# Gate and up of an inner tile as seven block products, and four rounds of inner tiles, in three feed-forward stages

## The chip, the cores and the metric

The kernel runs on one core of a Trainium2 chip. The metric is the device time of one execution in microseconds; three runs of the kernel before gave a median of 2734.63 us (2733.28 to 2737.92). The profile and the trace below come from one further execution with the profiler on.

## What is computed

Two transformer blocks on 512 tokens of width 1024, in float32. The first has two layers, and each layer has two feed-forward stages, one ahead of and one behind its mixing (a recurrent one in layer 0, windowed attention in layer 1). That makes four feed-forward stages, numbered 0 to 3. The second block follows stage 3. What matters here, cut from the reference:

```python
D_MODEL, SEQ, D_FF = 1024, 512, 2816

def swiglu(x, w_in, w_out):
    gate, up = jnp.split(x @ w_in, 2, axis=-1)
    return (jax.nn.silu(gate) * up) @ w_out

h = h + 0.5 * rms_norm(swiglu(rms_norm(h, g[0]), ffn_w_in[layer, 0], ffn_w_out[layer, 0]), g[1])
...
h = h + 0.5 * rms_norm(swiglu(rms_norm(h, g[4]), ffn_w_in[layer, 1], ffn_w_out[layer, 1]), g[5])
```

## The kernel before

Every large product keeps float32 accuracy by splitting both factors into a high part in the reduced format fp32r and a low rest. `weights` loads 128x1024 numbers of weights (512 KB, by a DMA issued on SyncE, into one of three raw buffers `wr`); ScalarE copies them to the high part (L153) and VectorE subtracts to get the low part (L154), both into one of five buffers `whl`. `mm3` then makes three matmuls for each block of weights: high by high, high by low, low by high (L164 to L166). Tokens lie along the free axis (512 columns, or two halves of 256), features along the partitions, in `KT` = 8 blocks of 128. The normalised tokens are held as `xn[k]`, scaled by the norm's gain and split; the norm's own factor per token, `rx`, is multiplied in behind the product.

`ffn` is one feed-forward stage; stages 0, 2 and 3 run through it (stage 1 is woven into the recurrent mixing by the class `Halves`, which stays). The 2816 inner features are 22 inner tiles of 128, worked in two rounds (`fh`) of `FH` = 11. An inner tile is gate and up: 2 x 8 blocks x 3 matmuls of 512 columns into two PSUM banks `gu`. `act` turns them into the inner activation: gate and up by `rx` on VectorE (L328, L329), Silu on ScalarE (L330), their product on VectorE (L331), and the split into `a` (L267 on ScalarE, L268 on VectorE). The first three tiles of a stage (`nsp`) run on the two token halves one after the other, since the second half of the tokens is still being normalised by the tail of the step before (`self.tail`).

After the eleven tiles of a round come the output products (`dtile`): 8 output tiles of 128 features, each 11 blocks x 3 matmuls into a PSUM bank `o`. Round 0 is copied by ScalarE into the buffers `m` (L393), round 1 is added to them by VectorE (L395), and the squares for the norm behind are summed. In round 1 the last five output tiles (four in stages 1 and 2) run on the two token halves apart, so that half 0 can be normed (`postnorm`, and then `after_half`: the next norm and the first work of the next stage) while TensorE makes half 1. The norm takes two small matmuls on TensorE: a sum over the partitions (`st<-ones,acc`, L175) and a spread of the factor (`st<-dg,ones`, L186).

Work of other stages that waits for nothing is fed in step by step as side generators (`ada` in stage 0; `kv_gain` and `angles` in stage 2). Each engine runs its instructions in order; the order is made by the scheduler of the Tile framework, which places the instructions that the code issues by a timeline of its own.

## Time and profile before

| | |
|---|---|
| median of 3 runs | 2734.63 us |
| profiled execution | 2736.7 us, of which the span is 2735.0 us |
| instructions | 43654 |
| TensorE busy | 2638.4 us, 96% |
| VectorE busy | 1472.2 us, 54% |
| ScalarE busy | 1154.1 us, 42% |
| GpSimd busy | 118.6 us, 4% |
| DMA | 344.2 MB, 126 GB/s over the span |

PE is TensorE, DVE is VectorE, ACT is ScalarE, POOL is GpSimd, SP is SyncE. Busy time is summed over the span. Matmuls are pipelined, so the durations that are listed for them overlap, and the distance of two starts says what one costs. A row of a stretch ends with the granted clock (1.00 is full), the DMAs' busy share and GB/s. In other rows, `out<-in` names the tiles, and L154 is line 154.

### The profile page before, as it was taken

To read this page: it belongs to the slowest core of one execution; us is meant where nothing else is said; L and a number is where in the kernel's file an instruction comes from. 1 tells how busy PE (TensorE), PEld (TensorE's weight loads), DVE (VectorE), ACT (ScalarE), POOL (GpSimd) and SP (SyncE) were. 2 spreads that over 40 slices of the span, in tenths; PEclk is the share of its full clock that TensorE was granted. 3 is DMA by queue.
4 is the path that set the end of the run, shared out by engine and by line. 5 is a ranking of instruction groups with operands and counts; after the bars stand their busy time and mean duration, and the time that the engine had idled before them with its cause. 6 is when DMAs were issued, how large, how long until landed. Compare 5 with 4: busy or idle time off the path is not lost.

```text
span 2735.0 us, 43654 instructions
## 1 busy us (share of the span) xinstructions
PE 2638.4 (96%) x17326; PEld 2288.5 (84%) x17326; DVE 1472.2 (54%) x2992; ACT 1154.1 (42%) x2061; POOL 118.6 (4%) x148
## 2 busy tenths in 40 slices
PE   8999988899999999999999999899999999999998
PEld 7888887778788999999988889679888898767777
DVE  7724456565548556448652446547524456235655
ACT  5223315345355554345532234446322334345542
POOL 0000000000000000000000000340000000001300
PEclk9999999999999999999999999999999999999999
DMA  6632316864666463235442333102323233113352
GB/s 206 213 109 93 108 49 217 239 186 136 184 196 169 131 205 127 93 109 179 131 149 94 99 109 128 47 24 87 114 93 97 96 103 122 54 52 100 116 184 82
DMA packets 207556, 344.20 MB, mean 126 GB/s; under 512 B 66164, under 2 KB 136180, under 8 KB 207352
## 3 DMA queue, kind: packets, MB, share of 16 engines
q1 hardware_dynamic: 206920, 341.13, 39.9%
q8 instruction: 136, 2.23, 0.4%
q14 instruction: 68, 0.56, 0.1%
q10 hardware_dynamic: 432, 0.28, 0.0%
HBM read 298.51 MB, written 41.26 MB: 124 GB/s over the span
## 4 chain that ended last, share of the span: by engine, by line
PE 85%; DVE 5%; DMA 4%; issue 3%; ACT 3%; SPq 0%; POOL 0%; DVEq 0%; ACTq 0%; POOLq 0%
PE gu L164 12%; PE gu L165 12%; PE gu L166 12%; PE o L164 8%; PE o L166 8%; PE o L165 8%; PE ps L594 4%; PE ps L164 2%; PE ps L166 2%; PE ps L165 2%; PE psg L164 1%; PE psg L166 1%; PE psg L165 1%; PE z L1783 1%; DMA kk<-kk 1%
## 5 line engine op out<-in xcount | busy, mean ns | idle before, releaser
L153 ACT ACTIVATE whl<-wr 128x1024 fp32r<-128x1024 f32 x417 | 439.7, 1059 | 727.9 <-PE gu L166 400.6
L154 DVE TENSOR_TENSOR whl<-wr,whl 128x1024 fp32r<-128x1024 f32 x417 | 508.2, 1222 | 368.3 <-ACT whl L153 367.4
L164 PE MATMUL gu<-xn,whl 128*128 128x512 f32 (+1 forms) x1200 | 436.2, 366 | 9.3 <-ACT xn L242 7.3
L165 PE MATMUL gu<-xn,whl 128*128 128x512 f32 (+1 forms) x1200 | 438.5, 366 | 3.1 <-DVE xn L243 2.9
L166 PE MATMUL gu<-xn,whl 128*128 128x512 f32 (+1 forms) x1200 | 437.5, 365 | 0.8 <-DVE whl L154 0.8
L166 PE MATMUL o<-a,whl 128*128 128x256 f32 (+1 forms) x906 | 297.7, 329 | 0.0
L165 PE MATMUL o<-a,whl 128*128 128x256 f32 (+1 forms) x906 | 296.8, 329 | 0.0
L164 PE MATMUL o<-a,whl 128*128 128x256 f32 (+1 forms) x906 | 296.3, 329 | 0.0
L164 PEld LDWEIGHTS gu<-xn,whl 128*128 128x128 f32 x1200 | 226.7, 190 | 45.3 <-ACT xn L242 7.5
L165 PEld LDWEIGHTS gu<-xn,whl 128*128 128x128 f32 x1200 | 227.5, 190 | 40.2 <-DVE xn L243 4.3
L166 PEld LDWEIGHTS gu<-xn,whl 128*128 128x128 f32 x1200 | 227.5, 190 | 37.0 <-DVE whl L154 1.2
L165 PE MATMUL gu<-pair,whl 128*128 128x256 f32 x704 | 200.2, 285 | 1.1 <-DVE pair L243 1.1
L166 PE MATMUL gu<-pair,whl 128*128 128x256 f32 x704 | 198.9, 283 | 1.2 <-DVE whl L154 1.2
L164 PE MATMUL gu<-pair,whl 128*128 128x256 f32 x704 | 199.0, 284 | 0.0
L165 PEld LDWEIGHTS o<-a,whl 128*128 128x128 f32 x906 | 170.7, 189 | 17.1
L166 PEld LDWEIGHTS o<-a,whl 128*128 128x128 f32 x906 | 170.6, 189 | 17.0
L164 PEld LDWEIGHTS o<-a,whl 128*128 128x128 f32 x906 | 170.3, 189 | 17.1
L594 PE MATMUL ps<-mxe,wraw 128*128 128x256 f32 x544 | 147.8, 423 | 15.3 <-DVE pair L567 7.5
L594 PEld LDWEIGHTS ps<-mxe,wraw 128*128 128x128 f32 x544 | 110.9, 212 | 39.0 <-DVE mxe L609 7.7
L165 PEld LDWEIGHTS gu<-pair,whl 128*128 128x128 f32 x704 | 133.2, 189 | 2.4 <-DVE pair L243 1.7
L166 PEld LDWEIGHTS gu<-pair,whl 128*128 128x128 f32 x704 | 133.6, 190 | 2.0 <-DVE whl L154 1.4
L164 PEld LDWEIGHTS gu<-pair,whl 128*128 128x128 f32 x704 | 132.6, 189 | 1.0
(436 smaller groups left out, 4737.1 us busy)
## 6 DMA issues: line engine op xcount, KB each, us to landing
wr<-in_ffn_w_in_dram SPq DMA_DIRECT2D x204, 512.0 KB, 3.5
wr<-in_ffn_w_out_dram SPq DMA_DIRECT2D x99, 512.0 KB, 3.5
wr<-in_w_in_dram SPq DMA_DIRECT2D x38, 512.0 KB, 3.5
wraw<-in_w_rkvo_dram SPq DMA_DIRECT2D x32, 512.0 KB, 4.2
wr<-in_w_rkvo_dram SPq DMA_DIRECT2D x32, 512.0 KB, 4.4
wr<-in_w_ada_dram SPq DMA_DIRECT2D x24, 512.0 KB, 4.4
wr<-in_w_qo_dram SPq DMA_DIRECT2D x16, 512.0 KB, 3.4
gates<-xf SPq DMA_DIRECT2D x48, 128.0 KB, 1.8
```

The costliest lines, as they stand in the source:

```text
L153: nc.scalar.activation(out=hl[:, 0, :cols], in_=raw[:, :cols], func=AF.Copy)
L154: nc.vector.tensor_tensor(out=hl[:, 1, :cols], in0=raw[:, :cols], in1=hl[:, 0, :cols].bitcast(F32), op=ALU.subtract)
L164: nc.tensor.matmul(ps, lhsT=wh, rhs=xh, start=start, stop=False, **k)
L165: nc.tensor.matmul(ps, lhsT=wh, rhs=xl, start=False, stop=False, **k)
L166: nc.tensor.matmul(ps, lhsT=wl, rhs=xh, start=False, stop=stop, **k)
L594: nc.tensor.matmul(ps, lhsT=w[:, b * P:(b + 1) * P], rhs=x, start=start, stop=stop)
L1783: nc.tensor.matmul(seg(z, i, j), lhsT=ntri if j == i else none, rhs=seg(hl[:, x], j), start=False, stop=x == 1 and j == 3, skip_group_chec ...
```

## The change

In stages 0, 2 and 3 gate and up of an inner tile become one product of two by two blocks. The weights are A = [[A11, A12], [A21, A22]] with gate as the upper row and up as the lower, and the two halves of the 1024 input features as columns; the tokens are X with the halves of the features as rows and the halves of the tokens as columns. Eight block products are replaced by seven, of which three take sums of weights (S1 to S4) or of tokens (X of `token_sums`) as factors. A block product is 4 blocks x 3 matmuls of 256 columns, so a tile takes 84 of them. The first three tiles of a stage are made as before.

`weight_sums` loads gate and up as before, forms four sums of 128x512 on GpSimd and splits 3.5 x 1024 columns in place of 2 x 1024; `token_sums` forms and splits the sums of tokens once per stage, for four values of k. In `hidden` the product accumulates in the bank `p` over A11, S2, S3 and A22 and is copied out by ScalarE in between, while `q` takes A12, S1 and S4; VectorE adds the copies, and the product of Silu and up moves to GpSimd. The last two block products of a tile are issued within the next tile, or between the first three output tiles.

The 22 inner tiles run in four rounds of 6, 5, 6 and 5, each followed by its output products, of which the last three rounds add to `m` on VectorE. The first three output tiles start without the round's last inner tile. The buffers `a` go from 12 to 7, `wx` is gone, `wq` (half as wide) is new, as are the buffers of the sums. `ada` works on 1024 columns at once, in a buffer of its own. The layout of `ffn_w_out` in memory follows the rounds.

```diff
+ROUNDS = (6, 5, 6, 5)
...
-            ap = self.pool("a", 12, es, side="right")
+            ap = self.pool("a", 7, es, side="right")
             tp = self.sg = self.pool("sg", 2, es, side="right")
-            wx = self.pool("wx", 2, es, side="right")
+            wq = self.pool("wq", 2, es, side="right")
+            one = self.pool("fx", 1, es, side="right")
+            self.room = lambda: one.tile([P, 4, 256], F32, tag="side", name="side")
+            sums = lambda j: one.tile([P, 4, 256], F32, tag=f"sum{j}", name="sum")
...
+            def token_sums():
+                for k in range(4):
+                    t = sums(k % 2)
+                    x11 = self.small.tile([P, 256], F32, tag="xf", name="xf")
+                    h = lambda i, j: self.h[:, k + 4 * i, 256 * j:256 * j + 256]
+                    g = lambda i: self.vecs[:, gcol + k + 4 * i:gcol + k + 4 * i + 1]
+                    sub = lambda o, i, j, x: nc.vector.scalar_tensor_tensor(out=o, in0=h(i, j), scalar=g(i), in1=x, op0=ALU.mult, op1=ALU.subtract)
+                    nc.scalar.activation(out=x11, in_=h(0, 0), func=AF.Copy, scale=g(0))
+                    sub(t[:, 0], 0, 1, x11)
+                    sub(t[:, 1], 1, 1, t[:, 0])
+                    nc.gpsimd.tensor_tensor(out=t[:, 2], in0=t[:, 1], in1=x11, op=ALU.subtract)
+                    sub(t[:, 3], 1, 0, t[:, 1])
+                    X[k] = one.tile([P, 2, 4, 256], F32R, tag=f"X{k}", name="X")
+                    nc.scalar.activation(out=X[k][:, 0], in_=t, func=AF.Copy)
+                    nc.vector.tensor_tensor(out=X[k][:, 1], in0=t, in1=X[k][:, 0].bitcast(F32), op=ALU.subtract)
...
+            def weight_sums(f):
+                G, U = (self.wraw.tile([P, 1024], F32, tag="wraw", name="wr") for _ in range(2))
+                nc.sync.dma_start(out=G, in_=win[2 * f])
+                nc.sync.dma_start(out=U, in_=win[2 * f + 1])
+                sa, sb = (sums(j).rearrange("p a b -> p (a b)") for j in range(2))
+                tt = lambda o, x, y, op: nc.gpsimd.tensor_tensor(out=o, in0=x, in1=y, op=op)
+                L, R = slice(0, T), slice(T, 2 * T)
+                w = {}
+                hg = split_w(G, big())
+                tt(sa[:, L], U[:, L], U[:, R], ALU.add)
+                tt(sa[:, R], sa[:, L], G[:, L], ALU.subtract)
+                ha = split_w(sa, big())
+                tt(sb[:, L], G[:, L], U[:, L], ALU.subtract)
+                tt(sb[:, R], G[:, R], sa[:, R], ALU.subtract)
+                h22 = split_w(U[:, R], wq.tile([P, 2, T], F32R, tag="wq", name="wq"))
+                hb = split_w(sb, big())
+                return dict(A11=(hg, 0), A12=(hg, 4), A22=(h22, 0), S1=(ha, 0), S2=(ha, 4), S3=(hb, 0), S4=(hb, 4))
...
+            def product(ps, w, x, start=False):
+                w, b = w
+                for k in range(4):
+                    if isinstance(x, tuple):
+                        i, j = x
+                        xh, xl = (self.xn[k + 4 * i][:, q, 256 * j:256 * j + 256] for q in range(2))
+                    else:
+                        xh, xl = (X[k][:, q, x] for q in range(2))
+                    self.mmhl(ps, w, b + k, xh, xl, start and k == 0, k == 3, skip_group_check=True)
+            def hidden(f, av):
+                w = weight_sums(f)
+                p, q = (self.mm.tile([P, 2, 256], F32, tag="mm", name="gu") for _ in range(2))
+                s, u = (tp.tile([P, 2, 256], F32, tag=x, name=x) for x in ("s", "av"))
+                cp = lambda o, x: nc.scalar.activation(out=o, in_=x, func=AF.Copy)
+                tt = lambda o, x, y, op, e=nc.vector: e.tensor_tensor(out=o, in0=x, in1=y, op=op)
+                r = self.rx.rearrange("p (h t) -> p h t", h=2)
+                product(p[:, 0], w["A11"], (0, 0), True)
+                cp(s[:, 0], p[:, 0])
+                product(q[:, 0], w["A12"], (1, 0), True)
+                yield
+                product(p[:, 0], w["S2"], 1)
+                cp(s[:, 1], p[:, 0])
+                yield
+                product(q[:, 1], w["S1"], 0)
+                product(p[:, 0], w["S3"], 2)
+                cp(u[:, 1], p[:, 0])
+                tt(u[:, 1], q[:, 1], u[:, 1], ALU.add)
+                tt(u[:, 1], u[:, 1], r[:, 1], ALU.mult)
+                yield
+                product(p[:, 0], w["A22"], 3)
+                tt(u[:, 0], p[:, 0], r[:, 0], ALU.mult)
+                yield
+                product(q[:, 1], w["S4"], (1, 1))
+                tt(s, q, s, ALU.add)
+                tt(s, s, r, ALU.mult)
+                nc.scalar.activation(out=s, in_=s, func=AF.Silu)
+                tt(u, s, u, ALU.mult, nc.gpsimd)
+                self.split(u.rearrange("p h t -> p (h t)"), av, 0, T)
...
+            f0 = 0
+            for rd, nf in enumerate(ROUNDS):
+                fs = list(range(f0, f0 + nf))
+                a = {}
+                last = rd == len(ROUNDS) - 1
+                if rd == 0:
+                    first_tiles(fs[:nsp], a)
+                prev = iter(())
+                for f in fs[nsp if rd == 0 else 0:]:
                     a[f] = ap.tile([P, 2, T], F32R, tag="a", name="a")
-                    w = [self.weights(win[2 * f + j]) for j in range(2)]
-                    gu = [self.mm.tile([P, T], F32, tag="mm", name="gu") for _ in range(2)]
-                    for j in range(2):
-                        for k in range(KT):
-                            self.mm3(gu[j], w[j], k, self.xn[k], 0, T, k == 0, k == KT - 1)
-                    act(f, *gu, 0, T)
-                    if fh == 0:
-                        for g in side:
-                            next(g, None)
-                if fh == 0:
-                    for g in side:
-                        run(g)
+                    g = hidden(f, a[f])
+                    next(g)
+                    next(prev, None)
+                    next(g)
+                    next(prev, None)
+                    next(g)
+                    prev = g
+                    for s in side:
...
+                head = []
+                for d in range(3):
+                    head.append(bank())
+                    part(head[d], d, 0, T, 0, nf - 1)
+                    next(prev, None)
+                for d in range(3):
+                    part(head[d], d, 0, T, nf - 1, nf)
+                    evict(head[d], d, 0, T)
+                if not last:
+                    for d in range(3, KT):
+                        ps = bank()
+                        part(ps, d, 0, T, 0, nf)
+                        evict(ps, d, 0, T)
```

On VectorE, in the middle of stage 3 before the change, this is one inner tile (`whl` are the weights' low parts, `s` and `av` the gate and up branch):

```order
L328 TENSOR_TENSOR s<-gu,rx 128x512
L154 TENSOR_TENSOR whl<-wr,whl 128x1024
L329 TENSOR_TENSOR av<-gu,rx 128x512
L331 TENSOR_TENSOR av<-s,av 128x512
L154 TENSOR_TENSOR whl<-wr,whl 128x1024
L268 TENSOR_TENSOR a<-av,a 128x512
```

In the change, at the end of a round of stage 3, the output tiles are added to `m`; `sum` and `wq` are factors of the next round's inner tiles:

```order
L506 TENSOR_TENSOR m<-o,m 128x256 x6
L156 TENSOR_TENSOR whl<-wr,whl 128x1024
L506 TENSOR_TENSOR m<-o,m 128x256 x4
L351 TENSOR_TENSOR whl<-wr,whl 128x1024
L506 TENSOR_TENSOR m<-o,m 128x256 x2
L351 TENSOR_TENSOR whl<-sum,whl 128x1024 x2
L351 TENSOR_TENSOR whl<-wr,whl 128x1024
L351 TENSOR_TENSOR wq<-wr,wq 128x512
L506 TENSOR_TENSOR m<-o,m 128x256 x4
L351 TENSOR_TENSOR whl<-sum,whl 128x1024 x2
L351 TENSOR_TENSOR whl<-wr,whl 128x1024
```

The splits of two inner tiles (twice `whl<-wr`, two of `sum`, and `wq<-wr`) now stand among the output tiles of the round before; in the tile itself, two splits stood between the four operations of `act`.

On GpSimd, which had nothing in these stages, this is what one inner tile has there in the change, ahead of its product of Silu and up (with the buffers' numbers, since the rows would read alike otherwise):

```order
L363 TENSOR_TENSOR sum_23540<-wr_23537 128x512
L363 TENSOR_TENSOR sum_23540<-sum_23540,wr_23536 128x512
L363 TENSOR_TENSOR sum_23541<-wr_23536,wr_23537 128x512
L363 TENSOR_TENSOR sum_23541<-wr_23536,sum_23540 128x512
L392 TENSOR_TENSOR av_23223<-s_23222,av_23223 128x512
L363 TENSOR_TENSOR sum_23663<-wr_23660 128x512
L363 TENSOR_TENSOR sum_23663<-sum_23663,wr_23659 128x512
L363 TENSOR_TENSOR sum_23664<-wr_23659,wr_23660 128x512
L363 TENSOR_TENSOR sum_23664<-wr_23659,sum_23663 128x512
```

The first four rows are a tile's sums, the last four those of the next; the second and the fourth of a tile take the result of the first and the second. The sums stand on an engine of their own, and each pair of `wr` buffers stays in use until its fourth sum.

On TensorE, at the end of stage 3, the norm of token half 0 before the change stands among the output products of half 1:

```order
L164 MATMUL o<-a,whl 128x256
L165 MATMUL o<-a,whl 128x256
L186 MATMUL st<-dg,ones 128x256
L166 MATMUL o<-a,whl 128x256
L164 MATMUL o<-a,whl 128x256
L165 MATMUL o<-a,whl 128x256
```

In the change the last rows of stage 3 are:

```order
L167 MATMUL o<-a,whl 128x256
L168 MATMUL o<-a,whl 128x256
L177 MATMUL st<-ones,acc 128x1 x2
L188 MATMUL st<-dg,ones 128x256
L177 MATMUL st<-ones,m 128x1 x12
L177 MATMUL st<-ones,acc 128x1 x2
L177 MATMUL st<-ones,m 128x1 x4
L188 MATMUL st<-dg,ones 128x256
L166 MATMUL ps<-xn,whl 128x256 x5
L188 MATMUL st<-dg,ones 128x256
L167 MATMUL ps<-xn,whl 128x256
L168 MATMUL ps<-xn,whl 128x256
```

Both halves' sums (`acc`), the spreads of the factors (`dg`) and the sums for the next norm (`m`) now stand behind the last output product, and then the next step's products begin (`ps<-xn`).

## Rows read from the trace of the kernel before

**Rows 1.** The page: busy time with share of span and instructions; granted clock by slice.

```profile
PE 2638.4 (96%) x17326; PEld 2288.5 (84%) x17326; DVE 1472.2 (54%) x2992; ACT 1154.1 (42%) x2061; POOL 118.6 (4%) x148
...
PEclk9999999999999999999999999999999999999999
```

**Rows 2.** Stretches in stages 0, 3: length, busy us (count) of PE, PEld, DVE, ACT, POOL.

```profile
140.00:340.00 200.00, 200.00 (x883) 164.51 (x883) 78.19 (x89) 59.73 (x80) 0.00 (x0) 1.00 0.31 100
...
2010.00:2210.00 200.00, 200.00 (x903) 165.07 (x902) 79.11 (x94) 59.91 (x81) 0.00 (x0) 1.00 0.31 100
```

**Rows 3.** Timeline of TensorE: start us, us, engine, line, operation; first and last of 36 and 68.

```profile
29.74 0.28 PE L165 MATMUL gu<-xn,whl 128*128 128x256 f32 x1
...
33.90 0.28 PE L164 MATMUL gu<-xn,whl 128*128 128x256 f32 x1
...
59.75 0.39 PE L165 MATMUL gu<-xn,whl 128*128 128x512 f32 x1
...
74.94 0.39 PE L166 MATMUL gu<-xn,whl 128*128 128x512 f32 x1
```

**Rows 4.** Groups by line and form, VectorE and ScalarE: busy us, mean ns of one.

```profile
L154 DVE TENSOR_TENSOR whl<-wr,whl 128x1024 fp32r<-128x1024 f32 x417 | 508.2, 1222 | 368.3 <-ACT whl L153 367.4
...
L243 DVE SCALAR_TENSOR_TENSOR xn<-h,vecs,xn 128x256 fp32r<-128x256 f32 x64 | 29.5, 475 | 0.0
...
L153 ACT ACTIVATE whl<-wr 128x1024 fp32r<-128x1024 f32 x417 | 439.7, 1059 | 727.9 <-PE gu L166 400.6 <-PE o L166 155.7 <-DMA wr<-in_ffn_w_in_dram 49.5
...
L393 ACT ACTIVATE m<-o 128x256 f32<-128x256 f32 x48 | 15.8, 380 | 52.8 <-PE o L166 52.8
```

**Rows 5.** Timeline of two stretches in which GpSimd and VectorE work at once.

```profile
612.30 0.54 DVE L1121 TENSOR_TENSOR wl<-wl,tt 64x48 f32<-64x48 f32 x1
...
613.55 0.19 DVE L1121 TENSOR_TENSOR wl<-wl,tt 64x39 f32<-64x39 f32 x1
...
852.46 1.54 POOL L1198 TENSOR_TENSOR sp<-S,pcol 64x256 f32<-64x256 f32 x2 [5.30 <-DVE mv L1250]
...
852.69 0.83 DVE L243 SCALAR_TENSOR_TENSOR pair<-h,vecs,pair 128x256 fp32r<-128x256 f32 x1
853.45 0.83 DVE L286 TENSOR_TENSOR h<-h,xf 128x256 f32<-128x256 f32 x1
```

**Rows 6.** GpSimd: its group by form, and four of it in a row in the timeline.

```profile
L1198 POOL TENSOR_TENSOR sp<-S,pcol 64x256 f32<-64x256 f32 x24 | 16.2, 677 | 29.7 <-DVE S L1233 23.2 <-DVE mv L1250 5.3
...
786.50 2.91 POOL L1198 TENSOR_TENSOR sp<-S,pcol 64x256 f32<-64x256 f32 x4 [0.43 <-DVE S L1233]
```

**Rows 7.** The page: DMA issues, KB each, us from issue to landing.

```profile
wr<-in_ffn_w_in_dram SPq DMA_DIRECT2D x204, 512.0 KB, 3.5
```

**Rows 8.** Timeline at the end of stage 3: VectorE, then TensorE.

```profile
2222.79 0.42 DVE L395 TENSOR_TENSOR m<-o,m 128x256 f32<-128x256 f32 x1 [2.52 <-PE o L166]
...
2228.15 0.48 DVE L185 TENSOR_SCALAR dg<-ident,rn 128x128 f32<-128x128 f32 x2
...
2239.05 0.75 DVE L286 TENSOR_TENSOR h<-h,xf 128x256 f32<-128x256 f32 x2
...
2244.30 0.48 DVE L185 TENSOR_SCALAR dg<-ident,rn 128x128 f32<-128x128 f32 x2
...
2231.12 0.59 PE L186 MATMUL st<-dg,ones 128*128 128x256 f32 x2
...
2246.68 0.60 PE L186 MATMUL st<-dg,ones 128*128 128x256 f32 x2
2248.70 0.50 PE L164 MATMUL ps<-xn,whl 128*128 128x256 f32 x2 [1.42 <-ACT xn L1562]
```

**Rows 9.** Timeline at the end of stage 0: VectorE, then TensorE.

```profile
367.85 0.43 DVE L395 TENSOR_TENSOR m<-o,m 128x256 f32<-128x256 f32 x1 [2.52 <-PE o L166]
...
399.82 1.65 PE L594 MATMUL ps<-mxe,wraw 128*128 128x256 f32 x3 [7.50 <-DVE pair L567]
```

**Rows 10.** The same view for a stretch at the start of stage 2.

```profile
1300.00:1340.00 40.00, 40.00 (x335) 39.90 (x334) 29.50 (x65) 23.52 (x40) 0.00 (x0) 1.00 0.37 111
```

More of the change, by code (lines that the diff above doesn't have):

```diff
@@ L310, in store_h, with ffn @@
             self.nc.sync.dma_start(out=dst[k * P:(k + 1) * P, :], in_=self.h[:, k, :])
[L313 removed]
+    def ffn(self, idx, gcol, gpost, after_half, side=(), early=()):
         nc = self.nc
@@ L320, in ffn @@
             nsp = 3
-            for fh in range(2):
-                fs = list(range(fh * FH, fh * FH + FH))
-                a = {}
-                def act(f, g, u, t0, n):
-                    r = self.rx[:, t0:t0 + n]
-                    s, av = (tp.tile([P, n], F32, tag=q, name=q) for q in ("s", "av"))
-                    nc.vector.tensor_tensor(out=s, in0=g, in1=r, op=ALU.mult)
-                    nc.vector.tensor_tensor(out=av, in0=u, in1=r, op=ALU.mult)
-                    nc.scalar.activation(out=s, in_=s, func=AF.Silu)
-                    nc.vector.tensor_tensor(out=av, in0=s, in1=av, op=ALU.mult)
-                    self.split(av, a[f], t0, n)
-                first = fs[:nsp] if fh == 0 else []
+            m, pb = None, 0
@@ L369, in ffn @@
-                if fh == 0:
-                    for g in side:
-                        run(g)
+                                        mm(f, j, k)
+                    for f in fs:
+                        r = self.rx[:, t0:t0 + n]
+                        s, av = (tp.tile([P, n], F32, tag=q, name=q) for q in ("s", "av"))
+                        nc.vector.tensor_tensor(out=s, in0=ps[f][:, 0], in1=r, op=ALU.mult)
+                        nc.vector.tensor_tensor(out=av, in0=ps[f][:, 1], in1=r, op=ALU.mult)
+                        nc.scalar.activation(out=s, in_=s, func=AF.Silu)
+                        nc.vector.tensor_tensor(out=av, in0=s, in1=av, op=ALU.mult)
+                        self.split(av, a[f], t0, n)
@@ L1528, in ada @@
     for j in range(3):
-        acc = [mp.tile([P, 256], F32, tag="m", name="ada") for _ in range(4)]
+        acc = N.room()
+        flat = acc.rearrange("p a b -> p (a b)")
         for k in range(KT):
@@ L1564, in modnorm, with angles @@
         yield
-def angles(N, mp, dram, out):
+def angles(N, dram, out):
     nc = N.nc
-    room = [mp.tile([P, 256], F32, tag="m", name="ang") for _ in range(3)]
-    pi, pf, fr, a, b, c, acc, *sines, inv = (room[j // 4][:, 64 * (j % 4):64 * (j % 4) + 64] for j in range(11))
+    room = N.room()
+    pi, pf, fr, a, b, c, acc, *sines, inv = (room[:, j // 4, 64 * (j % 4):64 * (j % 4) + 64] for j in range(11))
     pi, inv = pi.bitcast(I32), inv[:, 0:1]
```

112 lines of the change are left out of this document (69 added, 43 removed).

## The prediction

> **What bounds the kernel now.** I read the page's busy times first: TensorE is busy 96% of the span, at the upper of its two clock levels throughout [rows 1]. Then the sums by stretch inside feed-forward stages 0 and 3: TensorE is busy 200.00 of 200.00 us in each, VectorE 78 to 79, ScalarE 60, GpSimd not at all [rows 2]. So inside these stages TensorE alone sets the pace, and idle time of the others is worth nothing. Next, the spacing of its products in the timeline, since their listed lengths overlap: 68 starts of 512 columns from 59.75 to 74.94 us, 0.2267 us each; 36 starts of 256 columns from 29.74 to 33.90 us, 0.1189 us each [rows 3]. A halved product costs 5% more than half. Last, the stage ends: there TensorE runs out of work and the chain of norm, sums and next mix decides [rows 8, 9].
>
> All sums are made against the profiled execution: 2736.7 us, of which 2735.0 are its span. The median of the runs is 2734.6, 2.1 lower, and I shift the result by that.
>
> **Products.** An inner tile now takes 48 products of 512 columns: 48 x 0.2267 = 10.88 us. The change makes it 7 x 12 = 84 of 256: 84 x 0.1189 = 9.99 us [rows 3]. That is 0.89 us less, for 19 of 22 tiles (the first three stay) in three stages, 57 tiles: **-51 us**. The output products that run in two halves (for five of eight output tiles, in stage 2 four) fall from 33 to 15 per tile; a pair of halves costs 2 x 0.1189 - 0.2267 = 0.011 us more than a whole, so 18 x 14 x 0.011 = **-3 us**. The DMAs stay: 44 + 22 transfers of 512 KB per stage, 3.5 us each [rows 7].
>
> **Work beside the products.** Per tile, VectorE's splits of weights rise from 2 to 3.5 x 1024 columns. One takes 1.22 us [rows 4]; in a row each overlaps the next by 0.09 (two of 256 take 0.75 where one takes 0.42 [rows 8]), so 1.13 at 1024 columns, 0.33 at 256 and 0.6 between for 512. The splits come to 3 x 1.13 + 0.6 = 4.0 us and the activation to 3 x 0.33 + 3 x 0.6 = 2.8: 6.8 us against 2 x 1.13 + 4 x 0.6 = 4.7 before. ScalarE: 3.5 x 1.06, three copies out of PSUM at 0.38 [rows 4], Silu and split of 512 at some 0.62 each: 6.1 us. Both lie under 9.99 us. New is GpSimd, five adds or products of 512 columns per tile. The nearest row has 256 columns and 0.68 us; four in a row take 2.91 us, 0.73 each [rows 6]. So 512 columns lie between 0.68 and 2 x 0.73 = 1.46 us; I take 1.2, since part of an operation is fixed: 6.0 us per tile. Alone it fits too.
>
> **GpSimd and VectorE together** do not: in the trace two VectorE operations of 256 columns take 0.83 us each beside a GpSimd pair, where one takes 0.48 [rows 4, 5], and their ends come 0.76 us apart, where 0.33 is usual [rows 8]. One of 64x48 takes 0.54 beside GpSimd and the like of it 0.19 right after [rows 5]. So one GpSimd operation of 256 columns cost VectorE 0.43 us; at 512 columns I take 0.85. If each of the five hits, VectorE needs 6.8 + 5 x 0.85 = 11.0 us per tile, over 9.99. But VectorE has three operations per tile with an input in PSUM (1.3 us), and the order shows that the weights of about two tiles per round are split while the outputs of the round before run, where VectorE has little to do. A round of six tiles then asks 4.3 x (4.0 + 4 x 0.85) + 6 x (2.8 + 0.85) + 2.5 x 1.13 for the first output pieces = 56.5 us, of 59.9. It just fits; the buffers let weights be 2 to 8 us early. Bounds of the price: below 0, since such slack can hide all of it, above 1.0 us per tile (11.0 - 9.99). I take 0.2, nearer the lower end because the round's sum is under TensorE's: 57 x 0.2 = **+11 us**.
>
> The Trainium skill ("SBUF — State Buffer", § Who interferes with whom) has a rule that speaks against this change: a VectorE operation with two SBUF inputs and a GpSimd operation that reads SBUF exclude each other for the whole instruction. By it the sum would lose its overlap; that is the first rival.
>
> **Round ends.** The last tile's activation must reach the output products: two VectorE operations (1.2), Silu (0.62), GpSimd (1.2), copy (0.63) and handovers, some 4.5 us. In rounds 1 to 3 at least 24 whole products (5.4 us) stand between; in the last, 24 halves (2.9 us), so 2 us per stage: **+6 us** (0 to 12).
>
> **Stage starts.** The sums of tokens add per stage VectorE 4 x (3 x 0.39 + 1.13) = 9.2 us (0.475 less the overlap for the 256-column form [rows 4]) to a stretch of 40 us where it is already busy 29.5 [rows 10]. They are due only with the fourth tile, and 38.7 of 40 just fits; GpSimd's four adds come on top. I take 2 us per stage: **+6 us** (0 to 15).
>
> **Stage ends.** This is the price I am surest of. The last round has 5 tiles, not 11, so after half 0 is finished only 75 halved products (8.9 us) run in place of 165 (19.6 us) while half 0's norms are made: 10.7 us less cover. In stage 3 the chain runs from the eviction at 2222.79 to the next stage's first product at 2248.70, 25.9 us [rows 8]. It partly waits behind products in TensorE's queue: 2231.12 for an input done at 2228.63, 2246.68 for one done at 2244.8 [rows 8]. With nothing else queued it needs some 15 us from its first matmul, but the order now puts that behind all outputs: 8.9 + 15 = 24, so 10.7 + 24 - 25.9 = +8. Stage 0 likewise (32.0 us from 367.85 to 399.82 [rows 9]): +7. Stage 2 has key and value products to fill in, up to +10.7 without them: +5. Together **+20 us** (8 to 32, the upper end being the lost cover of all three).
>
> Sum: -51 - 3 + 11 + 6 + 6 + 20 = -11; 2736.7 - 11 - 2.1 = **2724 us**, 0.4% faster. About 0.2% (5.5 us) is what a measurement of this kernel can tell from no change.
>
> **Rivals.**
> 1. *GpSimd and VectorE become the bound (slower).* For it: the collisions [rows 5]; against: the preparation in output rounds. If every GpSimd operation holds VectorE up, a tile takes 11.0 us, and if not even the PSUM operations overlap and GpSimd needs its full 1.2, 6.8 + 6.0 - 1.3 = 11.5. It decides from the point where a GpSimd operation costs VectorE over (9.99 - 6.8)/5 = 0.64 us with no tile prepared ahead. It falls on the tiles not prepared, about 13 per stage, 39: 39 x 1.0 to 1.5 = +39 to +59 in place of +11, so 2752 to 2772; I name 2762. This is what the skill's rule (the same page) would do here: the rows of collisions agree with it, and none shows GpSimd loaded so densely.
> 2. *All covered.* No stalls in tiles, rounds or starts, ends at 12: -54 + 12 - 2.1: 2693. For it: VectorE is 60% idle in these stages [rows 2]; against: the queues are in order, and the ends have no other work.
> 3. *A loop of buffers holds the tiles.* The third raw buffer lets a tile's second load start only after the fourth GpSimd sum of the tile before: 3.5 [rows 7] + 4 x 1.2 + waits for VectorE 4 x 0.4 = 9.9 us, equal to TensorE's 9.99. A little more, 0.7 us per tile over 39 tiles, is +27 for +11: 2740, no change.
>
> **How the numbers follow.** Forecast 0.47 (its own range 2710 to 2734, so most of it is faster by over 0.2%), rival 1 0.25, rival 2 0.13, rival 3 0.15. Faster: 0.37 + 0.13 = 0.50. Within 0.2%: 0.10 of the forecast and 0.07 of rival 3: 0.17. Slower: 0.25 + 0.08 = 0.33. The range leaves out the lower half of rival 2 and the top of rival 1: 2695 to 2770.
>
> **What would show it.** Right: TensorE's products at 0.119 us in the tiles, tile pitch 10.0 to 10.4 us, gaps of 10 to 16 us at the ends of stages 0 and 3 and small ones before the fourth tile. Wrong: a pitch of 11 us with VectorE's 1024-column operations stretched beyond 1.23 us (rival 1), waits for the weight DMAs or GpSimd's sums (rival 3), or stage ends no longer than now (rival 2).

## The result and the profile after

The change takes 2858.46 us, the median of 4 runs (2855.95 to 2859.84), beside 2733.95 us before it: a ratio of 1.0453, with a 95% interval of 1.0435 to 1.0471. It is slower by 124 us, where 2724 us were forecast and the range ended at 2770.

The page of the changed kernel, busy times, granted clock by slice, and the chain that ended last, by engine:

```profile
PE 2655.1 (93%) x19126; PEld 2383.7 (83%) x19126; DVE 1802.6 (63%) x3295; ACT 1309.3 (46%) x2373; POOL 620.2 (22%) x445
...
PEclk9999988988999999999999999799999998999999
...
PE 64%; DVE 12%; POOL 9%; DMA 8%; ACT 4%; issue 3%; SPq 0%; POOLq 0%; DVEq 0%; ACTq 0%
```

Against [rows 1], VectorE has gained 330 us of busy time and GpSimd 502. TensorE's busy time has hardly changed, but idle stretches and slices of lower clock have come in, four of them in the first half. TensorE's share of the chain, 85% before, is 64%.

The windows view of the changed kernel, for the third round of stage 2 (the stretch of 420 products of gate and up between two sets of output products), for stage 3 as far as its last output product, and for the end of stage 3:

```profile
core 0: us, PE busy (x) PEld busy (x) DVE busy (x) ACT busy (x) POOL busy (x), PEclk, DMA share, GB/s
...
1566.22:1622.84 56.62, 53.28 (x422) 52.87 (x421) 46.16 (x46) 26.32 (x40) 38.60 (x22) 0.94 0.30 93
1965.29:2353.74 388.45, 362.64 (x2506) 337.29 (x2505) 280.28 (x383) 176.17 (x289) 166.78 (x99) 0.97 0.30 90
2354.00:2373.00 19.00, 11.23 (x47) 9.66 (x47) 12.30 (x38) 8.27 (x19) 0.00 (x0) 0.60 0.49 138
```

In [rows 2] TensorE was busy throughout at full clock. The first stretch holds 420 products of 256 columns, as many as five of the round's six tiles have (the others stand among output products); they should take 50 us and take 56.6, or 11.3 us per tile, while neither VectorE (46.2) nor GpSimd (38.6) is busy throughout. So no single engine is the bound; the time goes in waits from one to the next.

To see where the 123 us between the two profiled spans came from, I cut both spans at the same points, by the starts of TensorE's instructions: the last output product of stages 0, 2 and 3, the first product behind each, and the first of stages 2 and 3.

| stretch, us | before | after | difference |
|---|---|---|---|
| stage 0, to its last output product | 392.0 | 412.2 | +20.2 |
| end of stage 0, to the mixing's first product | 7.8 | 22.0 | +14.2 |
| mixing and stage 1, to stage 2 | 906.4 | 929.6 | +23.2 |
| stage 2 | 367.5 | 388.4 | +20.9 |
| attention, with the end of stage 2 | 196.0 | 213.1 | +17.1 |
| stage 3 | 376.8 | 388.5 | +11.7 |
| end of stage 3 | 2.1 | 18.9 | +16.8 |
| second block | 486.3 | 485.4 | -0.9 |

Inside the stages I took from each distance of two starts what the first instruction costs at full clock (0.2267 us for 512 columns, 0.1189 for 256 [rows 3], and 0.02 for the few of one or two columns). The sum of these costs fell from 1092.6 to 1036.4 us over the three stages, by 56.2. What is left over is waiting and slow clock. It is summed up to a stage's first output product (starts), later next to products of gate and up (tiles), and among the output products (outputs):

| us in three stages | starts | tiles | outputs |
|---|---|---|---|
| before | 21.6 | 0.0 | 15.0 |
| after | 54.8 | 63.5 | 27.7 |

The groups by line and form of the changed kernel, busy us, mean ns of one, and the idle time ahead of them:

```profile
L363 POOL TENSOR_TENSOR sum<-wr 128x512 f32<-128x512 f32 x114 | 191.1, 1685 | 238.1 <-DMA wr<-in_ffn_w_in_dram 128.3 <-DVE whl L351 88.4 <-DVE s L392 6.7
L363 POOL TENSOR_TENSOR sum<-sum,wr 128x512 f32<-128x512 f32 x57 | 101.8, 1786 | 2.5
L363 POOL TENSOR_TENSOR sum<-wr,sum 128x512 f32<-128x512 f32 x57 | 97.8, 1716 | 2.0
L392 POOL TENSOR_TENSOR av<-s,av 128x512 f32<-128x512 f32 x57 | 96.9, 1700 | 296.7 <-ACT s L413 291.2 <-issue 5.6
...
L351 DVE TENSOR_TENSOR whl<-sum,whl 128x1024 fp32r<-128x1024 f32 x114 | 173.5, 1524 | 52.3 <-ACT whl L350 51.7
L351 DVE TENSOR_TENSOR whl<-wr,whl 128x1024 fp32r<-128x1024 f32 x57 | 99.9, 1753 | 6.4 <-ACT whl L350 6.4
...
L351 DVE TENSOR_TENSOR wq<-wr,wq 128x512 fp32r<-128x512 f32 x63 | 65.8, 1046 | 31.4 <-ACT wq L350 30.8
...
L392 DVE TENSOR_TENSOR s<-gu,s 128x512 f32<-128x512 f32 x57 | 39.1, 686 | 42.4 <-PE gu L168 42.3
```

A GpSimd operation of 512 columns takes 1.69 to 1.79 us. VectorE's splits beside them are longer than in [rows 4]: 1.52 to 1.75 for 1024 columns, 1.05 for 512. An operation of 512 columns with one input in PSUM (`s<-gu,s`) takes 0.69.

Timeline of the changed kernel at the start of stage 2, GpSimd, VectorE, ScalarE, TensorE:

```profile
1401.47 0.95 POOL L343 TENSOR_TENSOR sum<-sum,xf 128x256 f32<-128x256 f32 x1 [1.64 <-DVE sum L339]
1403.58 3.54 POOL L363 TENSOR_TENSOR sum<-wr 128x512 f32<-128x512 f32 x2 [1.16 <-DVE X L347]
...
1408.60 1.33 POOL L363 TENSOR_TENSOR sum<-wr,sum 128x512 f32<-128x512 f32 x1
...
1402.09 2.68 DVE L347 TENSOR_TENSOR X<-sum,X 128x1024 fp32r<-128x1024 f32 x2 [0.27 <-ACT X L346]
...
1409.73 1.05 ACT L350 ACTIVATE whl<-sum 128x1024 fp32r<-128x1024 f32 x1
...
1410.83 0.58 PE L166 MATMUL gu<-X,whl 128*128 128x256 f32 x1 [7.07 <-ACT whl L350]
```

This is the wait before the fourth tile. The sums of tokens and the sums of weights share the buffers `sum`, and GpSimd makes them in order. The weights' sums begin when VectorE has split the last but one of the tokens' sums, and take 6.3 us; ScalarE then splits, and TensorE, which has waited 7.07 us, goes on.

Timeline of the changed kernel between two tiles of the third round of stage 2, with the same engines:

```profile
1589.68 2.25 POOL L363 TENSOR_TENSOR sum<-wr,sum 128x512 f32<-128x512 f32 x1
1591.90 1.25 POOL L392 TENSOR_TENSOR av<-s,av 128x512 f32<-128x512 f32 x1
...
1599.17 1.74 POOL L363 TENSOR_TENSOR sum<-wr 128x512 f32<-128x512 f32 x1
1600.87 2.27 POOL L363 TENSOR_TENSOR sum<-wr,sum 128x512 f32<-128x512 f32 x1
...
1593.18 0.63 ACT L269 ACTIVATE a<-av 128x512 fp32r<-128x512 f32 x1 [3.80 <-POOL av L392]
1593.72 0.37 ACT L391 ACTIVATE s<-gu 128x256 f32<-128x256 f32 x1
...
1594.14 0.58 PE L166 MATMUL gu<-X,whl 128*128 128x256 f32 x1 [3.09 <-ACT s L391]
...
1599.68 2.31 DVE L351 TENSOR_TENSOR whl<-wr,whl 128x1024 fp32r<-128x1024 f32 x1
```

The product of Silu and up (L392 on GpSimd) stands behind the sums in GpSimd's queue. ScalarE's split of `a` waits 3.80 us for it, the copy of `gu` out of PSUM stands behind that split in ScalarE's queue, and TensorE waits 3.09 us for the copy. At 1599.68 one split on VectorE takes 2.31 us, beside two GpSimd sums of 1.74 and 2.27.

What keeps the pace there shows in the chain that ended last of that stretch (start, us, what):

```profile
1574.76 5.67 POOL sum L363 x3
...
1580.44 3.65 DMA wr<-in_ffn_w_in_dram
...
1584.26 2.34 POOL sum L363
...
1589.68 2.26 POOL sum L363
...
1591.96 3.59 DMA wr<-in_ffn_w_in_dram
...
1597.07 6.08 POOL sum L363 x3
1603.14 2.25 POOL av L392
```

It is a loop of loads and sums. A tile's load of `up` into a raw buffer `wr` starts at 1580.44 and at 1591.96, each time 0.02 us after the fourth sum of the tile before has ended, since that sum is the last to read the buffer. The load takes 3.6 us, and the next four sums, of which the first needs it, 7.7 and 7.4 us (1584.26 to 1591.94, 1595.71 to 1603.14). That makes 11.5 us from one load to the next, where TensorE's products of a tile make 9.99. Of the sums, those that VectorE does not hold up take 1.3 us, the others 2.2 to 2.3.

In the whole program TensorE's waits for the copies out of PSUM come to 23.2 us (`ACT s`) and 12.3 (`ACT av`); groups by form:

```profile
L166 PE MATMUL gu<-xn,whl 128*128 128x256 f32 x924 | 262.8, 288 | 12.1 <-ACT xn L244 6.8 <-ACT whl L350 3.2 <-DVE av L454 1.5
...
L166 PE MATMUL gu<-X,whl 128*128 128x256 f32 x684 | 199.1, 292 | 37.2 <-ACT s L391 23.2 <-ACT whl L350 14.0
...
L166 PE MATMUL gu<-X,wq 128*128 128x256 f32 x228 | 66.3, 291 | 12.5 <-ACT av L391 12.3
```

Timeline of the changed kernel at the end of stage 3, VectorE's last eviction of half 0, then TensorE:

```profile
2344.75 0.83 DVE L506 TENSOR_TENSOR m<-o,m 128x256 f32<-128x256 f32 x2
...
2354.22 0.61 PE L177 MATMUL st<-ones,acc 128*128 128x1 f32 x4 [0.20 <-DVE acc L233]
2358.36 1.19 PE L188 MATMUL st<-dg,ones 128*128 128x256 f32 x2 [3.53 <-ACT sq L232]
...
2370.31 1.19 PE L188 MATMUL st<-dg,ones 128*128 128x256 f32 x2 [1.18 <-DVE dg L187]
2372.62 0.80 PE L166 MATMUL ps<-xn,whl 128*128 128x256 f32 x2 [1.11 <-ACT xn L1697]
```

From that eviction, which ends at 2345.58, it takes 27 us to the next product; in [rows 8] it took 25.5 from the end of the eviction at 2222.79. The chain is about as long as before, but only 75 halved products stand beside it. From 2354 on TensorE does little more than the norm's small matmuls, and its clock is granted at 0.60 in the mean of that stretch.

### The profile page after: what moved, and what is told of

Same layout as the page of the kernel before. It is cut to its first block, busy times and chain, and to the rows that moved or that the text cites. A ratio compares the mean times of both kernels' runs of the same rounds, so it can differ in the third digit from the quotient of the medians.

```text
span 2858.0 us, 48303 instructions
## 1 busy us (share of the span) xinstructions
PE 2655.1 (93%) x19126; PEld 2383.7 (83%) x19126; DVE 1802.6 (63%) x3295; ACT 1309.3 (46%) x2373; POOL 620.2 (22%) x445
## 4 chain that ended last, share of the span: by engine, by line
PE 64%; DVE 12%; POOL 9%; DMA 8%; ACT 4%; issue 3%; SPq 0%; POOLq 0%; DVEq 0%; ACTq 0%
POOL sum L363 8%; PE gu L166 6%; PE gu L168 6%; PE gu L167 6%; PE o L166 6%; PE o L168 5%; PE o L167 5%; DMA wr<-in_ffn_w_in_dram 4%; PE ps L730 4%; PE ps L166 2%; DVE whl L351 2%; PE ps L167 2%; PE ps L168 2%; PE psg L166 1%; DVE whl L156 1%
## 5 line engine op out<-in xcount | busy, mean ns | idle before, releaser
L156 DVE TENSOR_TENSOR whl<-wr,whl 128x1024 fp32r<-128x1024 f32 x300 | 374.1, 1250 | 172.6 <-ACT whl L155 171.3
L155 ACT ACTIVATE whl<-wr 128x1024 fp32r<-128x1024 f32 x300 | 315.7, 1057 | 345.7 <-PE gu L168 162.3
L167 PE MATMUL o<-a,whl 128*128 128x512 f32 (+1 forms) x822 | 282.9, 345 | 0.0
L168 PE MATMUL o<-a,whl 128*128 128x512 f32 (+1 forms) x822 | 280.6, 346 | 2.4 <-DVE whl L156 2.4
L166 PE MATMUL o<-a,whl 128*128 128x512 f32 (+1 forms) x822 | 271.9, 348 | 10.4 <-ACT a L269 4.8
L166 PE MATMUL gu<-xn,whl 128*128 128x256 f32 x924 | 262.8, 288 | 12.1 <-ACT xn L244 6.8
L167 PE MATMUL gu<-xn,whl 128*128 128x256 f32 x924 | 265.1, 288 | 3.6 <-DVE xn L245 3.5
L168 PE MATMUL gu<-xn,whl 128*128 128x256 f32 x924 | 262.5, 288 | 5.6 <-DVE whl L351 3.7
L363 POOL TENSOR_TENSOR sum<-wr 128x512 f32<-128x512 f32 x114 | 191.1, 1685 | 238.1 <-DMA wr<-in_ffn_w_in_dram 128.3
L166 PE MATMUL gu<-X,whl 128*128 128x256 f32 x684 | 199.1, 292 | 37.2 <-ACT s L391 23.2
L351 DVE TENSOR_TENSOR whl<-sum,whl 128x1024 fp32r<-128x1024 f32 x114 | 173.5, 1524 | 52.3 <-ACT whl L350 51.7
L168 PE MATMUL gu<-X,whl 128*128 128x256 f32 x684 | 196.5, 290 | 4.5 <-DVE whl L351 4.5
L167 PE MATMUL gu<-X,whl 128*128 128x256 f32 x684 | 197.0, 289 | 0.0
L166 PEld LDWEIGHTS gu<-xn,whl 128*128 128x128 f32 x924 | 179.1, 195 | 14.5 <-ACT xn L244 7.3
L167 PEld LDWEIGHTS gu<-xn,whl 128*128 128x128 f32 x924 | 180.3, 195 | 6.0 <-DVE xn L245 4.8
L168 PEld LDWEIGHTS gu<-xn,whl 128*128 128x128 f32 x924 | 178.8, 195 | 7.8 <-DVE whl L351 5.6
L166 PEld LDWEIGHTS o<-a,whl 128*128 128x128 f32 x822 | 154.9, 190 | 30.8 <-ACT a L269 5.8
L168 PEld LDWEIGHTS o<-a,whl 128*128 128x128 f32 x822 | 155.2, 189 | 22.0 <-DVE whl L156 2.8
L167 PEld LDWEIGHTS o<-a,whl 128*128 128x128 f32 x822 | 155.1, 189 | 18.5
```

The source lines that it names most:

```text
L155: nc.scalar.activation(out=hl[:, 0, :cols], in_=raw[:, :cols], func=AF.Copy)
L156: nc.vector.tensor_tensor(out=hl[:, 1, :cols], in0=raw[:, :cols], in1=hl[:, 0, :cols].bitcast(F32), op=ALU.subtract)
L166: nc.tensor.matmul(ps, lhsT=wh, rhs=xh, start=start, stop=False, **k)
L167: nc.tensor.matmul(ps, lhsT=wh, rhs=xl, start=False, stop=False, **k)
L168: nc.tensor.matmul(ps, lhsT=wl, rhs=xh, start=False, stop=stop, **k)
L351: nc.vector.tensor_tensor(out=hl[:, 1], in0=x, in1=hl[:, 0].bitcast(F32), op=ALU.subtract)
```

## The experiments

**The short rounds alone.** Four rounds, and ordinary products in them:

```diff
-                    g = hidden(f, a[f])
...
+                    for j in range(2):
+                        for k in range(KT):
+                            self.mm3(gu[j], w[j], k, self.xn[k], 0, T, k == 0, k == KT - 1)
...
-                        token_sums()
```

> Four rounds, but gate and up as ordinary products, without the sums of tokens and weights. Theory R (the short last round takes the cover from the stage ends, whatever the products are): stage ends as long as in the change, TensorE's gap of some 20 us behind stages 0 and 3 stays, and 2780 to 2805 us. Theory G (what hurts are the sums on GpSimd, at the ends too, since they leave VectorE behind): within 10 us of the kernel before, 2725 to 2745 us.

2761.40 us against 2732.12 (ratio 1.0104, 1.0076 to 1.0131). The stages are 12 us shorter than before the change together, but the ends are long: 20.8 and 16.2 us, and the attention 208.6. That is 40 us more in the three ends, of the 48.1 that the change has; theory R holds for the ends, though the total lies under its range, because the stages gained. Timeline of TensorE at the end of stage 3 in this kernel:

```profile
2277.14 1.22 PE L166 MATMUL ps<-xn,whl 128*128 128x256 f32 x4 [1.12 <-ACT xn L1700]
```

The next product starts at 2277.14, and the last output product had started at 2260.95.

**Without the sums of weights.** The splits take the raw blocks:

```diff
-                ha = split_w(sa, big())
+                ha = split_w(U, big())
...
-                hb = split_w(sb, big())
+                hb = split_w(G, big())
```

> The seven products with the four sums of weights per tile left out (the raw blocks are split in their place; the product of Silu and up stays on GpSimd). Theory G: the waits within the inner tiles and before the fourth tile go, some 55 us, so 2795 to 2810 us, and VectorE's splits of 1024 columns are back at 1.25 us. Rival (the queue of ScalarE and the three raw buffers hold the tiles, not GpSimd): within 15 us of 2858 us.

2771.74 us (ratio 1.0135, 1.0113 to 1.0156), 87 us under the change where theory G said some 55. The waits in the tiles fall from 63.5 to 8.6 us, in the starts from 54.8 to 38.3; 15 us of the 87 stand in the mixing (914.5). Groups by form on VectorE:

```profile
L351 DVE TENSOR_TENSOR whl<-wr,whl 128x1024 fp32r<-128x1024 f32 x171 | 210.0, 1231 | 102.5 <-ACT whl L350 101.6
...
L351 DVE TENSOR_TENSOR wq<-wr,wq 128x512 fp32r<-128x512 f32 x63 | 43.1, 687 | 27.2 <-ACT wq L350 27.2
```

The splits are back at 1.23 and 0.69 us. Without the sums the raw buffers come free earlier too, so this run does not tell a busy GpSimd from the loop of loads and sums.

**All on VectorE.**

```diff
...
-                tt = lambda o, x, y, op: nc.gpsimd.tensor_tensor(out=o, in0=x, in1=y, op=op)
+                tt = lambda o, x, y, op: nc.vector.tensor_tensor(out=o, in0=x, in1=y, op=op)
...
-                tt(u, s, u, ALU.mult, nc.gpsimd)
+                tt(u, s, u, ALU.mult)
```

> The same sums and the product of Silu and up on VectorE in place of GpSimd. If the two engines shut each other out, 0.62 us on VectorE are cheaper than 1.7 us on GpSimd: faster than the change by 20 to 45 us, 2813 to 2838 us. If they ran side by side, VectorE with 9.8 us per tile of 9.99 becomes the bound: 2858 us or more.

2778.95 us (ratio 1.0168, 1.0151 to 1.0185), 80 us under the change, more than either theory said. The tiles' waits are 11.6 us, the starts' 54.4 as in the change. The windows view, the same 420 products of stage 2's third round:

```profile
1515.45:1565.95 50.50, 50.50 (x422) 50.29 (x421) 44.51 (x67) 25.65 (x38) 0.00 (x0) 1.00 0.33 105
```

The same work takes 50.5 us, with VectorE busy for 44.5 of them; with GpSimd's help it took 56.6.

**The change in stage 3 alone** (`ffn7` is the new function, `ffn` the old):

```diff
-        N.ffn(3, N.halfg[:, 88:96], spilling(lambda hf: modnorm(N, hf)))
+        N.ffn7(3, 80, N.halfg[:, 88:96], spilling(lambda hf: modnorm(N, hf)))
```

> The change in stage 3 alone; stages 0 and 2 as before. If each stage pays for itself: 28 us over the kernel before, 2762 us, and the mixings between stages 0 and 3 take as long as before (906 us from stage 0 to 2, 196 us from stage 2 to 3). If the loss came from something all over the program, a third of it: 2775 us.

2759.94 us (ratio 1.0123, 1.0079 to 1.0167), as the first theory said, though its four runs spread from 2752.83 to 2781.02 and the profiled one is the lowest. In that profile stage 3 and its end take 388.1 and 18.9 us, as in the change; TensorE's products in the mixing stand in the very order of before, and take 899.5 us.

**The fourth tile as before,** on top of all on VectorE:

```diff
+                    if f == nsp:
+                        w = [self.weights(win[2 * f + j]) for j in range(2)]
...
+                        continue
```

> As e3 (all sums on VectorE), and the fourth tile of a stage as ordinary products of 512 columns, so that the sums of tokens and of the first weights have 10.9 us more. If the wait before the fourth tile comes from the chain sums of tokens, sums of weights, split: the wait goes, 3 x (7 - 0.9) = 18 us, 2760 us. If VectorE is simply too busy at the start of a stage: the wait moves one tile on, within 6 us of e3, 2773 to 2785 us.

2782.64 us (ratio 1.0161, 1.0142 to 1.0181): the total does not move. The starts lose 38.9 in place of 54.4 us, so at the starts the first theory is right by size (15.5), though the three stages together are only 9.4 us shorter, since the outputs lose 4.9 us more and the ordinary products cost 2.7; and the mixing took 936.8 us in this profile, 24.7 more than in the one of the kernel it is compared with.

**The last round in halves,** on top of all on VectorE; every output tile of the last round is made for half 0 first:

```diff
+                hn = 256 if last else T
...
+                    part(head[d], d, 0, hn, 0, nf - 1)
...
+                        for d in range(3 if hf == 0 else 0, KT):
```

> As e3, and in the last round all eight output tiles run in two halves, so 120 halved products (14.3 us) in place of 75 (8.9 us) stand behind half 0 of the tokens. If cover is what the stage ends lack: each of the three ends shorter by some 5 us, 2763 to 2768 us. If the ends are set by what VectorE and ScalarE have queued there (the five pieces of output weights now hold all five buffers until the end, so the next weights come later): no gain or a loss, 2777 to 2790 us.

2783.02 us (ratio 1.0168, 1.0151 to 1.0185), which is the second theory's total. The ends became shorter, more than forecast: 12.2 us (22.0), 13.1 (18.9), and the attention 202.6 (211.3). But stage 3 took 3.5 us more, the second block 9.6, the mixing 15.2. So the cover is what the ends lack. The largest part of what came back, 15.2 us, stands in the mixing, where TensorE's products have the same order as with the fourth tile as before (936.8 us there); that the longer cover caused it is not shown.

**The product of Silu and up on VectorE,** the sums on GpSimd:

```diff
-                tt(u, s, u, ALU.mult, nc.gpsimd)
+                tt(u, s, u, ALU.mult)
```

> The change with the product of Silu and up on VectorE, the sums of weights staying on GpSimd. If the waits within the tiles come from the chain behind that product (GpSimd's queue, then the split of a in ScalarE's queue, then the copies out of PSUM behind it): most of the waits inside rounds 2 to 4 go, some 40 us, 2815 us. If the sums themselves hold the tiles: under 15 us, 2845 to 2858 us.

2817.81 us (ratio 1.0285, 1.0249 to 1.0320), 40 us under the change. The total fits the first theory, its reason only in part: the tiles' waits fall by 18.5 us, to 45.0, the outputs' by 12.3, and the mixing was 11.2 shorter. With nothing but the sums on GpSimd, 45.0 us in the tiles are left. The loop of loads and sums is still there: in the third round of stage 2 the loads of `up` start at 1542.50, 1553.84 and 1564.84, 11.3 and 11.0 us apart, and between them the chain that ended last holds sums and loads alone; of that chain:

```profile
1553.84 3.63 DMA wr<-in_ffn_w_in_dram
...
1564.84 3.35 DMA wr<-in_ffn_w_in_dram
```

**As many sums that nobody reads,** on top of the kernel without the sums of weights:

```diff
+                        nc.gpsimd.tensor_tensor(out=t[:, q], in0=self.rx, in1=self.rx, op=ALU.add)
...
-                ha = split_w(sa, big())
+                ha = split_w(U, big())
```

> As e2 (the raw blocks are split, the sums of weights left out), but GpSimd makes as many sums of 128x512 of the norm's factor into a buffer that nothing reads. So GpSimd is as busy beside VectorE, and no product waits for it except through its queue. If the two engines' sharing alone slows VectorE enough: waits inside the tiles near those of the change (63.5 us in three stages), 2820 us or more. If the waits come from what depends on the sums (raw buffers, splits): near e2, 2772 to 2785 us.

2811.31 us (ratio 1.0276, 1.0249 to 1.0303), between the two. The tiles' waits are 44.6 us, against 8.6 with GpSimd free of sums. Groups by form on GpSimd and VectorE:

```profile
L368 POOL TENSOR_TENSOR sum<-rx 128x512 f32<-128x512 f32 x228 | 338.8, 1519 | 25.9 <-ACT rx L190 22.4 <-DVE X L347 3.1
...
L351 DVE TENSOR_TENSOR whl<-wr,whl 128x1024 fp32r<-128x1024 f32 x171 | 241.6, 1420 | 73.8 <-ACT whl L350 73.2
...
L351 DVE TENSOR_TENSOR wq<-wr,wq 128x512 fp32r<-128x512 f32 x63 | 52.9, 842 | 27.6 <-ACT wq L350 27.6
```

VectorE's splits are slow again, with no data going from one engine to the other in the sums. So GpSimd busy beside VectorE, with the product of Silu and up in its queue behind the sums, is enough for a loss of this size, without any wait for a sum; how much each of these two has of it, this run does not tell. But the waits are not those of the change. TensorE's groups by form in this kernel:

```profile
L166 PE MATMUL gu<-xn,whl 128*128 128x256 f32 x924 | 266.9, 293 | 28.9 <-ACT whl L350 10.9 <-ACT xn L244 6.8 <-DVE av L390 5.9
...
L166 PE MATMUL gu<-X,whl 128*128 128x256 f32 x684 | 193.2, 286 | 12.2 <-ACT s L389 8.9 <-ACT X L346 3.3
```

The wait for the copy `s` falls from 23.2 to 8.9 us, and that for new weights' splits (`ACT whl`, ahead of the products that take `xn`) rises from 3.2 to 10.9. So this run does not show that the change lost its time in this way.

**Two phases.** All on VectorE; rounds of 6 and 5 with seven products (the fourth tile as before), then a round of 11 ordinary tiles in the memory of the sums:

```diff
-ROUNDS = (6, 5, 6, 5)
+ROUNDS = (6, 5, 11)
...
+                if last:
+                    ph.close()
+                    ap = self.pool("b", 12, es, side="right")
```

> Seven products in rounds of 6 and 5 tiles alone (the first four tiles of the stage as ordinary products), all sums on VectorE, and then one last round of 11 ordinary tiles, which takes over the memory of the sums. If the short last round is what lengthens the stage ends: ends as before the change (7.8 and 2 us), and the products of 7 tiles per stage gain 3 x 6.2 us, of which the starts give back up to 15: 2718 to 2733 us. If the ends are long for another reason (the norm's order among the last outputs): 2755 us or more.

2755.24 us (ratio 1.0074, 1.0046 to 1.0103). The ends are those of before, 7.8 and 2.1 us, and the attention takes 194.2; timeline of TensorE at the end of stage 3:

```profile
2264.17 0.28 PE L168 MATMUL o<-a,whl 128*128 128x256 f32 x1
2264.28 0.60 PE L188 MATMUL st<-dg,ones 128*128 128x256 f32 x2
2266.30 0.85 PE L166 MATMUL ps<-xn,whl 128*128 128x256 f32 x5 [1.42 <-ACT xn L1718]
```

The spread `dg` stands right behind the last output product, and the next stage's product comes 2 us later. So the ends hang on the last round: short it brings them (the short rounds alone), long, with its buffers and order of before, it takes them away. The total is over the range of the first theory and in that of the second, whose reason the ends refute; it is so by stage 0 (399.7 us, 7.7 more than before) and the mixing (919.2).

**Later, in two stages.** Stage 0 as before; in stages 2 and 3 five ordinary tiles, six with seven products, eleven ordinary ones; the sums of tokens are made after the fourth tile:

```diff
-ROUNDS = (6, 5, 6, 5)
+ROUNDS = (5, 6, 11)
...
+                    if rd == 0 or last:
...
+                        if f == nsp:
+                            token_sums()
```

> Stage 0 as before the change; in stages 2 and 3 rounds of 5 ordinary tiles, 6 tiles with seven products (sums on VectorE) and 11 ordinary tiles, the sums of tokens made after the fourth tile. If what is left of the loss in e9 is the start of a stage and the new order of the mixing between stages 0 and 2: the starts cost nothing, the mixing stands as before, and 6 tiles x 0.89 us in two stages gain 10.7 us: 2718 to 2728 us, faster than before. If seven products bring waits wherever they stand: 2733 us or more.

2731.26 us against 2735.89 (12 and 17 runs), a ratio of 0.9979 with an interval of 0.9962 to 0.9995: faster than the kernel before by 0.2%, less than forecast and at the edge of what these runs can tell. The windows of stages 2 and 3:

```profile
1304.94:1669.38 364.44, 363.24 (x2096) 319.88 (x2094) 221.42 (x360) 150.66 (x236) 0.00 (x0) 1.00 0.34 110
1863.83:2235.82 371.99, 368.51 (x2166) 326.31 (x2165) 225.97 (x376) 149.69 (x238) 0.00 (x0) 1.00 0.30 97
```

They took 367.5 and 376.8 us before: 3.1 and 4.8 us less. The products gain 10.7 us in the two; in stage 2 2.3 us go in the tiles.

**Later, in three stages.** The same edit with stage 0 too.

> The same in stages 0, 2 and 3. By the first theory another 5.3 us less inside stage 0, 2713 to 2723 us, unless the mixing behind it gets another order and another time (it took from 898 to 937 us in the runs so far): then up to 2750 us.

2746.98 us (ratio 1.0039, 1.0023 to 1.0054). Stage 0 takes 396.8 us, 4.8 more than before, and the mixing 922.0. In stage 0 the starts are cheap (9.5 us), but the tiles lose 9.8 and the outputs 11.4. `ada`, VectorE's side work, runs only there; it was not taken out, so that it is the cause stays a guess.

**The change once more,** without an edit.

> The change once more, unaltered, for a second profile: the mixing between stages 0 and 2 is code that the change does not touch, but its instructions stand in another order there. If that order costs time by itself, it takes again 925 to 935 us. If the 929.6 us of the first profile were the scatter of the clock, it lies elsewhere in 898 to 920 us. The stages and their ends should repeat within 3 us.

2852.94 us (2 runs; ratio 1.0437, 1.0400 to 1.0475). TensorE's products in the mixing stand in the same order in both profiles, and took 929.6 and 919.6 us; the order of before took 906.4 and 899.5. So one order scatters by 7 to 10 us, and the new one was slower by some 20 in these four profiles. Two more orders were profiled twice: 907.4 and 898.1 us (the short rounds alone, the idle sums), 936.8 and 927.3 (the fourth tile as before, the last round in halves). The scatter within an order is 7 to 10 us each time, and the orders lie up to 30 apart, so the time goes with the order; what in it costs time, no run shows. Neither reading of the expectation is right alone. The stages repeat within 3 us, the ends behind stages 0 and 3 exactly, and the attention took 210.1 us (213.1).

## Why the prediction was wrong

- **Products.** Right: -54 us forecast (51 and 3), -56.2 measured.
- **GpSimd and VectorE together: the step that failed.** "I take 0.2, nearer the lower end because the round's sum is under TensorE's": the tiles lost 63.5 us, 1.3 for each of the 48 tiles in rounds 2 to 4, for 11 forecast. The sum of VectorE's work was indeed under TensorE's (46.2 of 56.6 us). A sum of work does not see what waits for what: a tile's load waits for the fourth sum of the tile before, and its sums for the load, 11.0 to 11.5 us for 9.99 of products. The product of Silu and up, in the same queue behind the sums, hands the delay on to ScalarE's copies and so to TensorE. The price was also low: 1.2 us were taken for a GpSimd operation of 512 columns, where it takes about 1.3 undisturbed (rows at 1408.60 and 1591.90) and 1.7 in the mean; the upper bound, 1.46, was passed too. The price on VectorE was too high (0.85 us for each operation, where all VectorE's lengthening comes to some 2.1 us per tile: between this kernel and the one with all on VectorE, the five forms with both inputs in SBUF differ by 34.7, 30.4, 22.7, 14.3 and 19.3 us over 57 tiles). That the sums on GpSimd are the cause is shown: without them the tiles lose 8.6 us, on VectorE 11.6. With the sums alone on GpSimd they still lose 45.0, and the loop sets the pace there too. No run broke the loop with the sums left on GpSimd, as a fourth raw buffer might; so how much of the 63.5 us is the loop's, and how much that of the product's place in the queue and of VectorE's lengthening, stays open. The idle sums lost 44.6 us by other waits.
- The loop stood in the prediction as rival 3, with a chance of 0.15: "3.5 [rows 7] + 4 x 1.2 + waits for VectorE 4 x 0.4 = 9.9 us". Its load was right (3.6), its four sums were not (6.4 forecast, 7.0 to 7.7 in the stretch shown), so it was priced at +27 in place of 63.5. Rival 1 (0.25) was right on the collisions and, with 1.0 to 1.5 us per tile, on the size, but by VectorE as the bound, which at 46.2 of 56.6 us it was not. Both totals (2740 and 2762) rested on all the other steps.
- The Trainium skill ("SBUF — State Buffer", § Who interferes with whom) says that VectorE operations with two SBUF inputs contend with GpSimd operations that read SBUF, and that those with at most one, outside its two-port modes, do not. The trace agrees: `wq<-wr,wq` went from 0.69 us (without the sums) to 1.05, while `s<-gu,s`, of the same size and with an input in PSUM, stayed at 0.69.
- **Stage starts.** +6 forecast, +33.2 measured. "They are due only with the fourth tile, and 38.7 of 40 just fits" counted VectorE's time; the chain runs through shared buffers from the tokens' sums to the weights' sums. On VectorE the sums cost the same here (54.4 us), and an ordinary fourth tile takes 15.5 us off.
- **Round ends.** +6 forecast; the outputs lost 12.7 us more than before. 10.2 of it is in stage 0 alone, so it is not the same step at every round's end, as forecast; what holds the outputs there no run isolates.
- **Stage ends.** "This is the price I am surest of": right by its mechanism (the short rounds alone brought 39.7 us, the long last round took them away), mis-sized: +48.1 us (14.2, 17.1 and 16.8) for +20, beyond the 32 given as the upper end. In stage 3 the chain did not shrink to 24 us as forecast; it stayed at 27. VectorE and ScalarE have half 1's sums and the next weights to do in the same time, and TensorE runs it at a low clock (0.60); that these are the reasons is not shown. (Its terms as written, 10.7 + 24 - 25.9, give 8.8, not 8.) Stage 2 was furthest off, with 17.1 for 5.
- **What was not priced at all:** the mixing and stage 1, +23.2 us (13.2 in the second profile). The change does not touch that code, but the scheduler orders it anew. It did not run at the full clock before either (0.96 in the mean), so "the upper of its two clock levels throughout" holds for the stages [rows 2] and not for the whole span.

By these terms: -56.2 + 63.5 + 33.2 + 12.7 + 48.1 + 23.2 - 0.9 = 123.6 us, for 123.0 between the spans.

## What to carry to other kernels

That every engine's work fits under the bound's does not show that it is hidden: follow one tile's data through the in-order queues and the buffers, add up the loop that one buffer makes from its load to the operation that frees it, and compare that with the time of a tile. Helping a half idle VectorE with GpSimd made the tiles slower here, 56.6 us for 420 products against 50.5 with VectorE alone. A saving that is paid for with shorter rounds loses the cover of the stage's end: seven products paid only with a long last round, a start left alone, and the sums on VectorE, in two of the three stages, and then 0.2%.
